# Block 0 alone ahead, blocks 1 to 3 together, and gathered rows asked for earlier than they are used

## The chip, the cores and the metric

The kernel runs on one core of a Trainium2 chip. The metric is the device time of one launch in microseconds. Of the engines, PE is TensorE (matmuls and transposes), DVE is VectorE, ACT is ScalarE, POOL is GpSimd, which here only sends the gathers of expert rows, and SP is the engine whose queue sends nearly all other transfers. Each engine works through its own list of instructions in a fixed order; a wait in front of one instruction holds back everything behind it on that engine.

## The reference

One decoder block over 512 tokens of width 1024, in float32. Two mixers run on one projection, their outputs are merged, and a layer of 16384 one-neuron experts follows:

```
h    = rms_norm(x); parts = split(h @ w_in)
y_att = sparse attention: an indexer picks 128 causal keys a query, softmax over these
y_dn  = chunked gated DeltaNet (conv, l2 norm, decay, triangular solve, state over chunks)
merged = sigmoid(ga) * (y_att @ w_att) + sigmoid(gb) * (y_dn @ w_dn)
x    = x + merged @ w_o
h2   = rms_norm(x); q = h2 @ w_query              # 8 heads, 2 halves of 128
s    = q . sub_keys; top 16 of 128 in each half   # the "lists"
best 16 of the 256 sums -> expert number, gate = softmax(best)
x    = x + sum over 8 heads x 16 experts: gate * gelu(u[e] . h2) * v[e]
```

## The kernel before, in words

The 512 tokens are four blocks of 128. The last step, the experts, is done in two ways. Blocks 0 and 1 (`SINGLE`) fetch for each token and each of its 128 picks the row `u[e]`, and later the row `v[e]`: one gather brings one row for each of 128 tokens (128x1024 float32, 512 KB), so a block needs 128 gathers for u and 128 for v, 512 in all. VectorE then makes a dot product with `h2` (line 923, called the use of a u row) or adds the row times its coefficient to `x1` (line 934, the use of a v row). Blocks 2 and 3 (`WHOLE`) go over all 16384 experts densely: `dense_u` multiplies a 128x1024 tile `ut` with the transposed `hT1` of both blocks (8 matmuls of 256 columns), `spread` turns picks and gates into a dense table of gates in DRAM (`gd`), and `dense_v` multiplies the activations, times those gates, with the v tiles into the accumulators `acc`. Fifty-four of the 128 `dense_u` are made ahead of `dense_v`, the rest beside it.

In front of that lie four chains (two of `deltanet`, `indexer`, `attender`), which go over the blocks in order. Between their steps a filler (`fill`) hands out other work: the projections (`hr` is the normed input of blocks 1 to 3, transposed, so its matmuls have 384 columns), and then `path`, which is merge, `w_o`, second norm, queries, scores and lists of the blocks that it is given. `path` runs three times: for block 0 and for block 1 alone in `single(b)` inside the filler, and for blocks 2 and 3 together after the chains. `choose` makes the final 16 picks of a head out of the lists, by top-8 passes on VectorE.

What sets the order: the functions are generators, and how many steps of the filler go between two steps of the chains is a constant (`FILL_A`, `FILL_B`). In the filler every second step also emits one row (`STEPS`), in the last `path` every second step (`STEPS_E`), in `spread` four a chunk (`CHUNK_ROWS`), in `dense_v` a share that comes from the work done. The framework then fixes each engine's order once, when the program is built. `all_rows` gives out the rows: u of block 0, u of block 1, v of block 0, v of block 1, each with its gather and its use together. Until the chains are over a row has one of four buffers (`ROWS`), then also one of eight more (`MORE_ROWS`). The expert numbers are `eu` (line 902), from which the v rows are had by adding 1 in place once the u rows are through.

Of the kernel before, what the change touches and what calls it, by code (L numbers as in the profile page):

```python
# [32 lines left out]
SINGLE, WHOLE = (0, 1), (2, 3)  # L33
NU = len(WHOLE) * P

FILL_A = 1.6
FILL_B = 1.8
# [10 lines left out]
AHEAD = 40  # L48
# [4 lines left out]
ROWS, MORE_ROWS = 4, 8  # L53
STEPS, STEPS_E, CHUNK_ROWS = 2, 2, 4
# [5 lines left out]
CST = ["ident", "triu", "ones", "blk64", "causneg", "causbias"] + [f"m{k}" for k in range(6)]  # L60
# [3 lines left out]
def constants():  # L64
# [5 lines left out]
        "ones": r >= 0,  # L70
# [15 lines left out]
def tile_block(ctx, tc, x, xT0, xT1, w_in, sc_cols, sc_rows, w_br, w_o, w_q, subT, uT, uv, cst, iota, out, dbg=None):  # L86
# [44 lines left out]
    hr = hp.tile([P, 8, NX], F32, name="hr")  # L131
# [24 lines left out]
    ident, triu, ones, blk64 = cs("ident"), cs("triu"), cs("ones"), cs("blk64")  # L156
# [84 lines left out]
    rowv = cp.tile([P, 8 + D], F32, name="rowv")  # L241
    load(rowv, sc_rows.to_broadcast([P, 8 + D]))
    alog, dtb, n2g = rowv[:, 0:4], rowv[:, 4:8], rowv[:, 8:8 + D]
# [274 lines left out]
    def projections(part):  # L518
# [17 lines left out]
        yield from output_gates(1)  # L536
        yield from keys(1)
        yield from queries(1)
        for t in (8 * br + dt for dt in range(8) for br in range(2)):
# [193 lines left out]
    x1d = {b: dr.tile([P, D], F32, name=f"x1d{b}") for b in (*SINGLE, *WHOLE)}  # L733
    uv2 = uv.rearrange("e (t d) -> (e t) d", t=2)
    x1, h2, ex_u, act = {}, {}, {}, {}
# [3 lines left out]
    def path(bs, place, banks=("mm",)):  # L739
# [10 lines left out]
        m_ = place("m", None)  # L750
        for dt in range(8):
            s_ = tmp()
            part = lambda t, i: t[:, i * n * P:(i + 1) * n * P]
            if bs[0] == 0:
# [9 lines left out]
            else:  # L764
                for i in range(2):
                    load(part(s_, i), sgd[8 * i + dt][:, slice(c.start - P, c.stop - P)])
                S.activation(s_[:, :2 * n * P], s_[:, :2 * n * P], AF.Sigmoid)
            w = plain(w_br[dt])
            o = turn()
            for i, y in enumerate((qT, szT)):  # L770
                for k in range(4):
                    mm(part(o, i), w[:, 4 * i + k, :], y[:, k, c], k == 0, k == 3)
                    if n > 1 and k == 1:
                        yield
                yield
            V.tensor_tensor(s_[:, :2 * n * P], s_[:, :2 * n * P], o[:, :2 * n * P], op=ALU.mult)
# [168 lines left out]
    def fill():  # L945
# [3 lines left out]
        while True:  # L949
# [19 lines left out]
            if not active:  # L969
                yield  # L970
# [288 lines left out]
```

## Time and profile before

| | us |
|---|---|
| three runs: lowest, median, highest | 1860.33, 1864.8, 1871.26 |
| the profiled execution's own time | 1860.58 |
| its span, from the first instruction to the last | 1858.8 |
| TensorE busy, VectorE busy | 1678.5, 1332.8 |
| ScalarE busy, GpSimd busy | 573.6, 629.4 |

Busy times are sums over the whole span; what an engine is worth in one stage has to be read from a window of that stage. The program falls into seven stages: the chains with the projections until the first gather is asked for (0 to 453 us), the chains with gathers beside them (to 718), the path of blocks 2 and 3 (to 854), `choose` for block 2 (to 938), the spread of both (to 1140), a gap (to 1201), and `dense_v` (to 1854). The last 4.8 us store the result.

### The profile page before, as it was taken

What the parts mean: (1) busy time and instruction counts of PE and PEld (TensorE: products, weight loads), DVE (VectorE), ACT (ScalarE), POOL (GpSimd) and SP (SyncE); (2) the same over time, 40 slices, a digit from 0 to 9 for tenths busy, and PEclk for the clock granted to TensorE, in tenths of its full rate; (3) what the DMA queues carried; (4) which work ended last, traced back from release to release, by engine and by line L of the source; (5) the groups of instructions that cost most, each with busy time, mean ns of one, the idle gap of its engine ahead of it and who ended that gap; (6) DMA issues with size and microseconds to landing.
All of it is one profiled execution on the core that took longest, in us unless ns stands there. A gap on an engine that the chain in (4) does not pass through costs nothing.

```text
span 1858.8 us, 24234 instructions
## 1 busy us (share of the span) xinstructions
PE 1678.5 (90%) x8330; PEld 1311.6 (71%) x8330; DVE 1332.8 (72%) x3114; ACT 573.6 (31%) x1165; POOL 629.4 (34%) x516
## 2 busy tenths in 40 slices
PE   6899999899999968895379997699999999999998
PEld 5766686776667766495269996477777777777766
DVE  3733563978678899789996877886865856567675
ACT  5255322221136314011056885011212222122222
POOL 0000000001542443446834435554533533343430
PEclk8999999999998987997779999799999999999999
DMA  5422355343998899999979999999998999999985
GB/s 212 137 102 74 111 193 195 100 142 106 338 328 319 310 361 336 363 343 360 366 271 343 359 366 389 412 409 409 404 373 325 410 354 365 395 365 362 383 312 170
DMA packets 190123, 556.30 MB, mean 299 GB/s; under 512 B 17840, under 2 KB 63664, under 8 KB 187952
## 3 DMA queue, kind: packets, MB, share of 16 engines
q1 hardware_dynamic: 116272, 286.28, 42.4%
q0 software_dynamic: 73728, 268.47, 38.3%
q8 instruction: 66, 1.08, 0.2%
q14 instruction: 57, 0.47, 0.1%
HBM read 528.60 MB, written 25.95 MB: 298 GB/s over the span
## 4 chain that ended last, share of the span: by engine, by line
PE 54%; DVE 15%; issue 12%; DMA 11%; POOL 5%; ACT 2%; DVEq 0%; POOLq 0%; SPq 0%; ACTq 0%
PE acc L94 18%; PE mm L94 14%; DMA row<-in_uv_dram,eu 9%; PE dn L94 5%; POOL row L913 4%; DVE row L923 3%; PE at L94 3%; DVE wk L573 1%; DVE m L572 1%; DMA row__9423<-in_uv_dram,eu 1%; DMA row__8663<-in_uv_dram,eu 1%; DMA row__7536<-in_uv_dram,eu 0%; DMA row__7605<-in_uv_dram,eu 0%; PE at L609 0%; DMA C<-in_cst_dram 0%
## 5 line engine op out<-in xcount | busy, mean ns | idle before, releaser
L913 POOL DMA_INDIRECT row<-in_uv_dram,eu x318 | 386.3, 1215 | 933.0 <-DVE eu L902 455.3
L923 DVE CUSTOM_DVE_ANT_0 row<-row,h 128x1024 f32<-128x1024 f32 x233 | 281.5, 1217 | 59.4 <-DMA row<-in_uv_dram,eu 58.6
L94 PE MATMUL mm<-hT,ut 128*128 128x256 f32 x864 | 204.5, 394 | 64.4 <-ACT ge L1058 34.2
L94 PE MATMUL mm<-hr,wt 128*128 128x384 f32 (+1 forms) x688 | 241.2, 490 | 0.0
L94 PEld LDWEIGHTS mm<-hT,ut 128*128 128x128 f32 x864 | 168.1, 199 | 89.7 <-ACT ge L1058 35.0
L180 DVE TENSOR_TENSOR vl<-vt,vh 128x1024 fp32r<-128x1024 f32 x86 | 104.0, 1220 | 103.9 <-ACT vh L179 103.8
L94 PEld LDWEIGHTS mm<-hr,wt 128*128 128x128 f32 x688 | 122.9, 190 | 75.9 <-issue 8.6
L94 PE MATMUL acc<-vt,ge 128*128 128x512 f32 x336 | 151.0, 592 | 0.0
L94 PE MATMUL acc<-vl,ch 128*128 128x512 f32 x344 | 139.6, 406 | 6.5 <-DVE vl L180 6.5
L94 PE MATMUL acc<-vh,cl 128*128 128x512 f32 x344 | 135.7, 394 | 0.0
L94 PE MATMUL acc<-vh,ch 128*128 128x512 f32 x344 | 121.9, 437 | 3.8 <-ACT gs L1054 3.8
L179 ACT CAST vh<-vt 128x1024 fp32r<-128x1024 f32 x86 | 88.1, 1044 | 85.7 <-DMA vt<-in_uv_dram 85.1
L934 DVE SCALAR_TENSOR_TENSOR x1s<-row,act,x1s 128x1024 f32<-128x1024 f32 x85 | 109.0, 1282 | 3.0 <-DMA row<-in_uv_dram,eu 1.3
L180 DVE TENSOR_TENSOR cl<-gt,ch 128x256 fp32r<-128x256 f32 x86 | 36.3, 423 | 101.2 <-ACT ch L179 97.9
L94 PEld LDWEIGHTS acc<-vt,ge 128*128 128x128 f32 x336 | 63.8, 190 | 62.6 <-issue 60.3
L179 ACT CAST ch<-gt 128x256 fp32r<-128x256 f32 x86 | 34.7, 404 | 231.9 <-PE acc L94 221.8
L94 PE MATMUL mm<-h,wt 128*128 128x128 f32 x624 | 82.4, 291 | 7.2 <-DVE h L202 4.3
L94 PEld LDWEIGHTS mm<-h,wt 128*128 128x128 f32 x624 | 79.3, 206 | 10.8 <-DVE h L202 4.6
L1098 ACT ACTIVATE ob<-ob,sl 128x128 f32<-128x128 f32 x256 | 78.2, 388 | 26.2 <-DVE ob L1095 26.2
L94 PEld LDWEIGHTS acc<-vh,ch 128*128 128x128 f32 x344 | 66.0, 192 | 26.0 <-issue 8.6
L94 PEld LDWEIGHTS acc<-vl,ch 128*128 128x128 f32 x344 | 65.3, 190 | 22.1 <-DVE vl L180 8.2
L94 PE MATMUL mm<-hT,wt 128*128 128x128 f32 x640 | 79.8, 284 | 1.0 <-ACT tmp L849 1.0
(988 smaller groups left out, 3189.8 us busy)
## 6 DMA issues: line engine op xcount, KB each, us to landing
ut<-in_uT_dram SPq DMA_DIRECT2D x128, 512.0 KB
vt<-in_uv_dram SPq DMA_DIRECT2D x128, 512.0 KB
wt<-in_w_in_dram SPq DMA_DIRECT2D x82, 512.0 KB
wt<-in_w_q_dram SPq DMA_DIRECT2D x48, 512.0 KB
gd<-gb SPq DMA_DIRECT2D x16, 1024.0 KB
gt<-gd SPq DMA_DIRECT2D x16, 1024.0 KB
wt<-in_w_br_dram SPq DMA_DIRECT2D x24, 512.0 KB
wt<-in_w_o_dram SPq DMA_DIRECT2D x24, 512.0 KB
```

Of the source, the lines that this page charges most:

```text
L94: hop[0] = PE.matmul(o, l, r, start=start, stop=stop).ins
L179: S.copy(hi, src)
L180: return V.tensor_tensor(lo, src, hi.bitcast(F32), op=ALU.subtract).ins
L572: V.max(m8, src[:, :N])
L573: V.match_replace(wk[:, :N], m8, src[:, :N], TAKEN)
L913: G.indirect_dma_start(out=r, out_offset=None, in_=uv2, in_offset=bass.IndirectOffsetOnAxis(ap=ix, axis=0))
L923: V.tensor_tensor_reduce(r, r, h2[b], 1.0, 0.0, op0=ALU.mult, op1=ALU.add, accum_out=act[b][:, s:s + 1])
L934: V.scalar_tensor_tensor(x1[b], r, act[b][:, s:s + 1], x1[b], op0=ALU.mult, op1=ALU.add)
L1098: S.activation(ob[:, t], ob[:, t], AF.Copy, scale=sl[:, 2, n:n + 1])
```

## The change

- `path` runs twice, for block 0 alone and for blocks 1 to 3 together. `single(1)` is gone from the filler, so `w_br`, `w_o` and `w_q` are loaded twice and not three times; matmuls of the later `path` have 384 columns where they had 256, and 128 in `single(1)`.
- In the filler, block 0's `path` goes ahead of all projections once its chains are done, and until then the filler gets fewer steps (`FILL_0` 0.9 where it was 1.6).
- Rows are handed out in the order block 0 u, block 0 v, block 1 u, block 1 v, 0.3 a step of the filler, and each gather is emitted three (later seven) rows ahead of the use that belongs to it. There are five buffers, later six more a ring. The numbers of the v rows are a table of their own.
- Block 1's scores are kept; its lists, its `choose` and its expert numbers are written behind the spread of blocks 2 and 3 in the program.
- 52 `dense_u` are made ahead instead of 54; eight of these are left until behind the spread in the program.
- `norm2`'s gain is loaded into `h2` and not held all the time; `x1` of blocks 0 and 1 stays in SBUF.

The diff, cut to its core:

```
+OTHERS = (1, 2, 3)
-FILL_A = 1.6
-FILL_B = 1.8
+FILL_0, FILL_A, FILL_B = 0.9, 1.6, 1.8
-AHEAD = 40
+AHEAD = 38
-ROWS, MORE_ROWS = 4, 8
-STEPS, STEPS_E, CHUNK_ROWS = 2, 2, 4
+ROWS, MORE_ROWS = 5, 6
+PACE, STEPS_E, CHUNK_ROWS = 0.3, 3, 4
+LAGS = 3, 7
+LAST_U = 8
...
     def path(bs, place, banks=("mm",)):
...
             w = plain(w_br[dt])
-            o = turn()
+            ss = []
             for i, y in enumerate((qT, szT)):
+                s_ = tmp()[:, :N]
+                load(s_, sgd[8 * i + dt])
+                S.activation(s_, s_, AF.Sigmoid)
+                o = turn()[:, :N]
                 for k in range(4):
-                    mm(part(o, i), w[:, 4 * i + k, :], y[:, k, c], k == 0, k == 3)
+                    mm(o, w[:, 4 * i + k, :], y[:, k, c], k == 0, k == 3)
...
+                if n == 1 or b in WHOLE:
+                    lists(b, h, sc, place("sr", b))
+                else:
+                    kept[h] = sc
...
     def all_rows():
-
+        coming = []
         for b in SINGLE:
             while b not in act:
                 yield
-            for s in range(P):
-                r = row_of(ex_u[b][:, s:s + 1])
-                V.tensor_tensor_reduce(r, r, h2[b], 1.0, 0.0, ...)
-                emitted[0] += 1
-                yield
-        for b in SINGLE:
...
+            for second in range(2):
+                for s in range(P):
+                    coming.append((b, second, s, row_of(places[b][second][:, s:s + 1])))
+                    emitted[0] += 1
+                    if len(coming) > LAGS[len(rings) > 1]:
+                        use(*coming.pop(0))
+                    yield
+        for c in coming:
+            use(*c)
...
     def fill():
...
+            if alone is None and done >= {("y", 0, i) for i in range(3)}:
+                alone = single(0)
+            if SINGLE[0] in act:
+                due += PACE
+                while due >= 1.0:
+                    due -= 1.0
+                    rows()
+            if alone is not None and next(alone, True) is None:
+                pass
+            elif others and next(others[0], True):
+                others.pop(0)
+            yield
...
-            due += FILL_A if ("attention", 1) not in done else FILL_B
+            due += FILL_0 if ("y", 0, 0) not in done or ("y", 0, 1) not in done else FILL_A if ("attention", 1) not in done else FILL_B
...
-    while SINGLE[-1] not in act:
+    while SINGLE[0] not in act:
         next(filler)
...
-    for n, _ in enumerate(path(WHOLE, place, ("mm", "at", "dn0", "dn1"))):
+    for n, _ in enumerate(path(OTHERS, place, ("mm", "at", "dn0", "dn1"))):
...
-            dense(left * (NCH - n) // NCH)
+            dense(LAST_U + (left - LAST_U) * (NCH - n) // NCH)
             rows(CHUNK_ROWS)
+    dense(0)
+    b = SINGLE[1]
+    for h in range(8):
+        lists(b, h, kept[h], rp.tile([P, 2 * P], F32, name="sr1"))
+    choose(b, new)
+    indices(b, new, lp)
```

Three places where the order of instructions moves. VectorE, around the first expert numbers `eu0` and the first uses of u rows; before, rows (each with an instruction that reads its sum into `act0`) stand among single steps of the chains:

```order
L901 TENSOR_SCALAR area_2915<-area_2905 128x128
L902 SCALAR_TENSOR_TENSOR eu0_2991<-area_2905,area_2915 128x128
L923 ISA row_2995,act0_2994<-row_2995,h2_0_2093 128x1024
L923 ISA act0_2994 128x1
L923 ISA row_3038,act0_2994<-row_3038,h2_0_2093 128x1024
L923 ISA act0_2994 128x1
L923 ISA row_3051,act0_2994<-row_3051,h2_0_2093 128x1024
L923 ISA act0_2994 128x1
L417 TENSOR_TENSOR vb_3728<-dn0_3729,beta_139 128x256
L423 TENSOR_TENSOR attT_3767<-dn0_3768,dT_2999 128x256
L923 ISA row_3090,act0_2994<-row_3090,h2_0_2093 128x1024
L923 ISA act0_2994 128x1
```

After, a little behind `eu0`, the same engine has block 1's delta rule (`AT`, `am`, `XX`) between runs of rows:

```order
L954 ISA row_2330,act0_2258<-row_2330,h2_0_1716 128x1024
L954 ISA act0_2258 128x1
L385 TENSOR_TENSOR AT_2492<-dn1_2493,dT_2417 128x256
L391 TENSOR_TENSOR am_2514<-AT_2492,C_87 128x256
L393 TENSOR_TENSOR XX_2513<-C_87,am_2514 128x256
L954 ISA row_2336,act0_2258<-row_2336,h2_0_1716 128x1024
L954 ISA act0_2258 128x1
L954 ISA row_2356,act0_2258<-row_2356,h2_0_1716 128x1024
L954 ISA act0_2258 128x1
L954 ISA row_2363,act0_2258<-row_2363,h2_0_1716 128x1024
L954 ISA act0_2258 128x1
L954 ISA row_2400,act0_2258<-row_2400,h2_0_1716 128x1024
```

What moved is the point at which rows begin: `eu0` stands at row 778 of VectorE's order before and at row 528 after. From `eu0` to the last attention step of block 3 VectorE has 102 uses of rows before and 201 after.

TensorE, in the queries of the late path (`hT1` is its transposed, normed input, `sT` the keys of the scores); before, a query is done block by block:

```order
L94 MATMUL dn0_6264<-hT1_5619,wt_6265 128x128 x8
L94 MATMUL dn0_6264<-hT1_5619,wt_6267 128x128 x5
L94 MATMUL mm_6229<-sT_6225,qt_6227 128x128 x2
L94 MATMUL at_6248<-sT_6225,qt_6227 128x128 x2
L94 MATMUL dn0_6264<-hT1_5619,wt_6267 128x128 x3
L94 MATMUL dn0_6264<-hT1_5619,wt_6265 128x128 x8
L94 MATMUL dn0_6264<-hT1_5619,wt_6267 128x128 x8
```

After, one set of eight does three blocks:

```order
L98 MATMUL dn0_5836<-hT1_4985,wt_5838 128x384 x8
L98 MATMUL dn1_5837<-hT1_4985,wt_5851 128x384 x2
L98 MATMUL dn1_5796<-sT_5791,qt_5793 128x128
L98 MATMUL mm_5812<-sT_5791,qt_5793 128x128
L98 MATMUL at_5828<-sT_5791,qt_5793 128x128
L98 MATMUL dn1_5837<-hT1_4985,wt_5851 128x384 x6
```

The 256 narrow query matmuls of this path became 112 of 384 columns, 16 of 256 and 16 of 128.

VectorE where the spread starts (`oa`, `ob` are its one-hot tables); before, the rest of the second `choose` and uses of block 1's u rows (`act1`) follow the first tables:

```order
L1095 TENSOR_TENSOR oa_7303<-io_142,sl_7300 128x1024
L1095 TENSOR_TENSOR ob_7304<-io_142,sl_7300 128x1024
L1095 TENSOR_TENSOR oa_7327<-io_142,sl_7300 128x1024
L1095 TENSOR_TENSOR ob_7328<-io_142,sl_7300 128x1024
L704 TENSOR_SCALAR a__7987<-t1_7985 128x128
L709 TENSOR_SCALAR n__7996<-pf_7984 128x128
L692 TENSOR_REDUCE gs_7980<-gate3_5629 128x8
L923 ISA row_5861,act1_5191<-row_5861,h2_1_4401 128x1024
```

After, the same place has uses of block 0's v rows (into `x1_0`) and the candidate sums of block 1's `choose` (`ca` from `ts1`):

```order
L1121 TENSOR_TENSOR oa_6660<-io_144,sl_6657 128x1024
L1121 TENSOR_TENSOR ob_6661<-io_144,sl_6657 128x1024
L1121 TENSOR_TENSOR oa_6684<-io_144,sl_6657 128x1024
L1121 TENSOR_TENSOR ob_6685<-io_144,sl_6657 128x1024
L950 SCALAR_TENSOR_TENSOR x1_0_1715<-row__7381,act0_2258,x1_0_1715 128x1024
L693 MAX_INDEX bp_7215<-bs_7214,cr0_7252 128x8
L693 MAX_INDEX bp_7215<-bs_7214,cr1_7258 128x8
L695 TENSOR_TENSOR gate3_4994<-bs_7214 128x128
L677 TENSOR_TENSOR ca_8048<-ts1_5484 128x8x16
```

Block 1's `choose`, written behind the spread, was drawn into it, and the 256 rows of block 1 all stand behind it.

## Rows read from the trace of the kernel before

**Rows 1.** Windows of the seven stages; busy us and records of each engine.

```profile
core 0: us, PE busy (x) PEld busy (x) DVE busy (x) ACT busy (x) POOL busy (x), PEclk, DMA share, GB/s
0.00:453.00 453.00, 417.14 (x2355) 317.20 (x2356) 267.91 (x957) 155.73 (x313) 0.20 (x4) 0.97 0.40 135
453.00:718.00 265.00, 233.91 (x1256) 172.43 (x1255) 208.07 (x664) 88.52 (x180) 111.54 (x104) 0.92 0.91 327
718.00:854.00 136.00, 126.08 (x785) 105.68 (x785) 119.53 (x401) 20.65 (x39) 59.63 (x53) 0.95 0.95 346
854.00:938.00 84.00, 26.70 (x103) 21.39 (x102) 83.28 (x316) 7.89 (x15) 61.42 (x50) 0.68 0.94 354
938.00:1140.00 202.00, 196.34 (x1138) 179.25 (x1139) 163.02 (x222) 150.08 (x363) 93.06 (x68) 0.97 0.97 343
1140.00:1201.00 61.00, 35.56 (x149) 29.65 (x147) 44.39 (x48) 7.07 (x14) 34.48 (x29) 0.83 1.03 412
1201.00:1854.00 653.00, 642.65 (x2554) 485.98 (x2552) 445.35 (x510) 143.64 (x243) 269.08 (x212) 0.99 0.94 361
```

**Rows 2.** Timeline: start, length, engine, instruction, idle time before with its releaser.

```profile
409.43 0.61 PE L94 MATMUL mm<-tmp 128*128 128x128 f32 x4
...
455.17 0.29 DVE L902 SCALAR_TENSOR_TENSOR eu<-area 128x128 int32<-128x128 f32 x1
455.74 1.07 POOL L913 DMA_INDIRECT row<-in_uv_dram,eu  x1 [455.29 <-DVE eu L902]
...
461.26 1.22 DVE L923 CUSTOM_DVE_ANT_0 row<-row,h 128x1024 f32<-128x1024 f32 x1 [5.80 <-DMA row<-in_uv_dram,eu]
```

**Rows 3.** Groups of instructions: busy us, mean ns of one, idle before.

```profile
L923 DVE CUSTOM_DVE_ANT_0 row<-row,h 128x1024 f32<-128x1024 f32 x233 | 281.5, 1217 | 59.4 <-DMA row<-in_uv_dram,eu 58.6 <-issue 0.2
L94 PE MATMUL mm<-hT,ut 128*128 128x256 f32 x864 | 204.5, 394 | 64.4 <-ACT ge L1058 34.2 <-DMA ut<-in_uT_dram 30.2
L94 PE MATMUL mm<-hr,wt 128*128 128x384 f32 x496 | 173.9, 490 | 0.0
...
L934 DVE SCALAR_TENSOR_TENSOR x1s<-row,act,x1s 128x1024 f32<-128x1024 f32 x85 | 109.0, 1282 | 3.0 <-DMA row<-in_uv_dram,eu 1.3 <-DVE x1s L934 0.2
...
L94 PE MATMUL dn<-hT,wt 128*128 128x128 f32 x320 | 38.1, 279 | 0.0
L94 PE MATMUL mm<-wt,m 128*128 128x512 f32 x80 | 37.7, 596 | 0.0
```

**Rows 4.** Timeline of VectorE where uses of u rows follow each other directly.

```profile
892.89 1.22 DVE L923 CUSTOM_DVE_ANT_0 row__7761<-row__7761,h 128x1024 f32<-128x1024 f32 x1
894.04 0.08 DVE L923 DVE_READ_ACCUMULATOR2_ANT act<- 128x1 f32 x1
```

**Rows 5.** The same groups, VectorE up to 720 us: delta rule and top-8 passes.

```profile
L399 DVE TENSOR_TENSOR XX<-XX,dn 128x512 f32<-128x512 f32 x40 | 27.2, 681 | 19.1 <-PE dn L94 18.3 <-issue 0.6
L572 DVE MAX8 m<-wk 128x8 f32<-128x256 f32 (+2 forms) x45 | 24.9, 553 | 0.6
L573 DVE MATCH_REPLACE8 wk<-m,wk 128x256 f32<-128x256 f32 (+2 forms) x45 | 24.3, 540 | 0.0
```

**Rows 6.** Windows of 46 to 47 us; columns as in the first group.

```profile
650.00:696.00 46.00, 31.61 (x218) 28.43 (x219) 41.57 (x171) 5.43 (x15) 18.57 (x18) 0.87 0.98 362
696.00:743.00 47.00, 38.14 (x151) 30.38 (x150) 45.21 (x163) 19.24 (x27) 18.92 (x19) 0.70 0.94 336
882.00:929.00 47.00, 17.57 (x64) 14.02 (x62) 46.28 (x175) 4.30 (x7) 38.15 (x30) 0.72 0.97 366
```

**Rows 7.** Waits from 453 to 718 us: total us, times, longest.

```profile
POOL row L913 <- DVE act L923: 73.3, 42, 5.1
DVE row L923 <- DMA row<-in_uv_dram,eu: 42.0, 34, 5.8
```

**Rows 8.** Timeline in the gap between spread and `dense_v`, TensorE.

```profile
1170.99 12.51 PE L94 MATMUL mm<-hT,ut 128*128 128x256 f32 x48 [18.46 <-DMA ut<-in_uT_dram]
```

More of the change, by code (lines that the diff above doesn't have):

```diff
@@ L58 @@
 PLAIN = 3
-CST = ["ident", "triu", "ones", "blk64", "causneg", "causbias"] + [f"m{k}" for k in range(6)]
+CST = ["ident", "triu", "blk64", "causneg", "causbias"] + [f"m{k}" for k in range(6)]
 CI = {n: i for i, n in enumerate(CST)}
@@ L69, in constants @@
         "triu": r <= c,
-        "ones": r >= 0,
         "blk64": (r // 64) == (c // 64),
@@ L750, in path @@
         m_ = place("m", None)
+        N = n * P
         for dt in range(8):
-            s_ = tmp()
-            part = lambda t, i: t[:, i * n * P:(i + 1) * n * P]
-            if bs[0] == 0:
+            if n == 1:
+                s_, o = tmp(), None
+                part = lambda t, i: t[:, i * P:(i + 1) * P]
                 o = turn()
@@ L830, in path @@
         for h in range(8):
+            o = first_o
             if h:
-                o = turn()
-                w = [plain(w_q[2 * h + p]) for p in range(2)]
-                for j in range(n):
-                    for p in range(2):
-                        yield from query(o, w[p], j, p)
-            else:
-                o = first_o
+                o = [turn() for _ in range(2)] if n > 1 else [turn()] * 2
+                for p in range(2):
+                    yield from query(o, plain(w_q[2 * h + p]), p, slice(0, N))
             sT = place("sT", None)
@@ L914, in row_of, with use @@
         return r
+    def use(b, second, s, r):
+        a = act[b]
+        if second:
+            V.scalar_tensor_tensor(x1[b], r, a[:, s:s + 1], x1[b], op0=ALU.mult, op1=ALU.add)
+            if s == P - 1:
+                nc.sync.dma_start(out[col(b), :], x1[b])
+            return
+        V.tensor_tensor_reduce(r, r, h2[b], 1.0, 0.0, op0=ALU.mult, op1=ALU.add, accum_out=a[:, s:s + 1])
+        if s == P - 1:
+            S.activation(a, a, AF.Gelu)
+            V.tensor_tensor(a, a, flat(gate[b]), op=ALU.mult)
     def all_rows():
+        coming = []
         for b in SINGLE:
@@ L945, in fill @@
     def fill():
-        active, singles, n, b = [projections(0)], list(SINGLE), 0, None
-        nexts = [projections(1)]
+        others, alone, due = [projections(0), projections(1)], None, 0.0
         while True:
-            if b is None and singles and done >= {("y", singles[0], i) for i in range(3)} and (singles[0] == 0 or not nexts and len(active) == 0):
-                b = singles.pop(0)
-                active.append(single(b))
-            if nexts and len(active) == 0 or nexts and done >= {("z", 0)}:
-                active.insert(0, nexts.pop(0))
-            if SINGLE[0] in act and n % STEPS == 0:
-                rows()
-            n += 1
-            for g in active + active[1:]:
-                if g not in active:
-                    continue
-                try:
-                    next(g)
-                except StopIteration:
-                    active.remove(g)
-                    if b in act:
-                        b = None
-                    continue
-                yield
-            if not active:
-                yield
+            if alone is None and done >= {("y", 0, i) for i in range(3)}:
[9 more added lines that the diff above has]
+                others.pop(0)
+            yield
     sgd = [dr.tile([P, T - P], F32, name=f"sgd{t}") for t in range(16)]
```

122 lines of the change are left out of this document (63 added, 59 removed).

## The prediction

> **What bounds the kernel now.** First the windows by stage. Two stages are TensorE's almost alone, `dense_v` with 642.65 of 653 us and the spread with 196.34 of 202; in both VectorE has 40 to 200 us to spare. The path (718 to 854) is nearly so: 126.08 of 136. `choose` (854 to 938) is VectorE's: 83.28 of 84, TensorE 26.70. The gap (1140 to 1201) belongs to the transfers, 412 GB/s with TensorE at 35.56 of 61 [rows 1]; there the last `dense_u` wait 18.46 us for `ut` [rows 8]. The chain stage with rows (453 to 718) is mixed: TensorE 233.91 of 265 and VectorE 208.07, that is 88% and 79% [rows 1]. The finer windows say which of them is near its end: VectorE fills 90% of 650 to 696 and 96% of 696 to 743, TensorE 69% and 81% [rows 6]. So as soon as rows are dense, VectorE is what the chains wait for. The change leaves the late stages much as they are and doubles the rows in just this stage, so the question is what that does to the chains' end.
>
> **The change, part by part.** I set it against the profiled execution: 1858.8 us of span and 1.8 outside it, 1860.6, which is 4.2 under the median of the runs. Counts come from the two built orders, durations from the rows.
>
> *When rows can begin.* Before, the last score matmul of block 0 is at 409.43 and its numbers `eu` are ready at 455.17 + 0.29, 46 us later, filled with top-8 work [rows 2]. TensorE has fewer matmuls ahead of that score after: 72 of 384 columns and not 200, 214 small ones of the delta rule and not 312, 58 of attention and not 89. By 0.70 us each (173.9 over 248; a float32 matmul is two records) and 0.24 (38.1 over 160) [rows 3] that is 128 x 0.70 + 129 x 0.24 = 121 us of work; TensorE is busy 417.14 of 453 [rows 1], so 131 us of time. The score comes at 278, and the first request 46 later at about 325. The bounds are 300 (the 46 us shrink to 21, if block 0 is alone on VectorE) and 335 (no gain from the idle share).
>
> *The chains with rows beside them.* From `eu0` to the last attention step of block 3, VectorE's order holds 201 uses of rows after, 102 before. The 128 u rows cost 1.15 each (892.89 to 894.04 back to back [rows 4]), 147; the 73 v rows 1.28 [rows 3], 93. Since `eu0` stands earlier, 148 us of chain work now lie behind it too. Its largest term is the indexer's top-8 passes: 48 pairs at 0.553 + 0.540 [rows 5], less 0.07 of overlap an instruction, 46; then the delta rule at 48 (23 products `XX` at 0.68 are 16 of that [rows 5]), attention 16, small inverse roots 15, index sums 14, and 11 of the rest. The same way of counting gives 205 for the stretch before, where the trace has 208.07 [rows 1]. So VectorE has 147 + 93 + 148 = 388 us of work, while TensorE has some 305. At the share that VectorE reaches when rows are dense, 0.933 (41.57 + 45.21 over 93 [rows 6]), this takes 416 us, and the chains end at 325 + 416 = 741; before it was 718. At 0.99, which only `choose` has (46.28 of 47 [rows 6]), it is 717; at 0.90, 756. Filling `single(1)` out of this stage does take 59 us from TensorE, but TensorE isn't late here.
>
> *The gathers' latency.* A gather's use came 5.5 us after its request [rows 2], and before VectorE waited 42.0 us for rows in this stage, over about 100 of them, 0.4 each [rows 7]. Requests there waited 73.3 us for a buffer [rows 7]. Now a gather is asked for three rows ahead, into five buffers. If four rows of other work (4.6 us and more) lie between, little remains; if the wait stays, 201 x 0.4 = 80 us come on top. I take none at the forecast, since the shares above already hold a part of it, and keep 80 for the range. By the Trainium skill ("DMA: Bandwidth & Descriptors", Anatomy of one DMA, SWDGE path) such a transfer takes 2.0 us and its bytes at 436 GB/s, an estimate of 3.2 us for 512 KB. Five buffers would then hide it wholly. The trace's 5.5 us is over that, so the page does not settle it.
>
> *The path.* It now carries block 1 too. After the chains' end TensorE has 16 more `w_o` matmuls at 0.94 [rows 3], 15; queries of 112 x 0.70 + 16 x 0.474 + 16 x 0.24 = 90 where there were 256 x 0.24 = 61, 29; branches 48 x 0.70 against 64 x 0.474, 3; scores and transposes 6. That is 53 on a stage which TensorE fills to 93%: 136 + 53 = 189. Thirty-two weight loads of 512 KB fewer and 28 fewer gathers (53 GpSimd records before [rows 1]) leave the transfers lighter, but they weren't what was late.
>
> *`choose`.* The same VectorE work for two blocks with some 30 rows beside it, where there were about 41: 84 - 11 x 1.2, with 6 to 9 us back for the two heads' chains standing closer: 80. *The spread.* 296 `dense_u` matmuls beside it and not 312, -16 x 0.474 = -8; against it block 1's `choose`, some 17 us of VectorE, which has 39 idle now and 42 rows fewer, so nothing; ScalarE bunched at the end, +5. I take 200. *The gap.* It was long because gathers and the v tiles took the queues from the last `ut`. After, no row of block 1 is asked for until its numbers are there, behind the spread. I take 38 and keep 61 as a bound.
>
> *`dense_v`.* 576 `dense_u` matmuls and not 592, -8: 645 by TensorE. All 256 gathers of block 1 now lie here, where 212 did [rows 1]. The bytes are 361 x 0.653 = 236 MB before, plus 44 x 0.524, 258 MB: 626 us at the gap's 412 GB/s. It is close to the end of what is there; behind the last `dense_u`, some 109 us of TensorE have 58 MB to bring in, 141 us, of which buffers and an uneven order hide a part. I add 12: 657. The Trainium skill ("DMA: Bandwidth & Descriptors", Where 436 GB/s comes from) puts transfers between HBM and SBUF at about 358 GB/s. By that this stage would need 258 / 0.358 = 721 us. The trace says no: 412 over the whole gap, and 361 over `dense_v` itself.
>
> *Sum.* 741 + 189 + 80 + 200 + 38 + 657, with 4.8 behind it and 1.8 outside the span: 1911.6, say 1912. That is 51 over the profiled execution: +23 in the chains, +53 in the path, -25 in the four stages behind it. The work that `single(1)` did in idle time of a stage now stands where TensorE has none.
>
> **The rivals.**
> 1. *VectorE has more room than I give it.* If only TensorE's work counts, the chains end at 718 - 59 = 659 and the whole at 1830. For it: VectorE idles 57 us in the stage before. Against it: 388 us from 325 to 659 don't fit. It needs the first request at 300, a full VectorE (692) and 10 to 20 us won in the path by its lighter transfers: 1840 to 1855. Faster.
> 2. *It cancels.* The first request is at 300, VectorE at 0.99 throughout: 300 + 392 = 692, and the sum is 1863. No change that a measurement of this kernel can tell (within 0.5%, 1855.5 to 1874).
> 3. *The gathers make VectorE wait.* The 0.4 us of each row stays with five buffers, for all 201: the chains end at 325 + 388 + 80 = 793, and the time is 1964. For it: 42.0 us of waits before [rows 7], and 201 x 0.524 MB with the weights ask for about 330 GB/s over the stage, as much as the 327 of before. Against it: the requests are further ahead of the uses. With half of the wait it is 1935 to 1940.
> 4. *The end waits for transfers.* The 58 MB behind the last `dense_u` take their 141 us in full: 20 us on the forecast, 1932. Inside the range.
>
> **How the numbers follow.** The forecast (chains' end at 717 to 756) has 0.50, with 1885 to 1930 as its own range; rival 4 has 0.06, rival 3 0.17, rival 2 0.14 and rival 1 0.13. Slower by over 0.5% is forecast, 3 and 4: 0.73. Same 0.14, faster 0.13. The range of 8 in 10 leaves out the better part of rival 1 and the upper half of rival 3: 1850 to 1960.
>
> **What the profile after would show.** The first gather at 300 to 335 us. From there to the last attention copy VectorE at 90% or more and TensorE well under 80%, ended near 740. The next stage near 190 us, TensorE over 90%. A gap under 45 us, and `dense_v` with the transfers' share near 1.0 in its last quarter. The forecast is wrong if the chains end before 705 us, or if the path takes under 170; the size is wrong through rival 3 if VectorE's waits for rows are over 60 us before the chains end.

## The result, and the profile after

The changed kernel takes 1930.0 us (four runs, 1926.3 to 1933.3) against 1864.7 of the kernel before: a ratio of 1.035, with a 95% interval of 1.031 to 1.039. It is 3.5% slower. The forecast was 1912. The profiled execution took 1927.2 us over a span of 1925.3.

The windows by stage, cut at these events: first gather, last attention copy, last score, first and last spread matmul, first and last `acc`.

```profile
core 0: us, PE busy (x) PEld busy (x) DVE busy (x) ACT busy (x) POOL busy (x), PEclk, DMA share, GB/s
0.00:318.00 318.00, 287.01 (x1805) 237.40 (x1806) 168.78 (x662) 116.59 (x242) 0.20 (x4) 0.96 0.49 164
318.00:762.00 444.00, 353.36 (x1385) 228.21 (x1383) 387.84 (x872) 94.27 (x212) 230.40 (x206) 0.82 0.83 294
762.00:938.00 176.00, 172.45 (x600) 103.60 (x600) 74.25 (x396) 28.96 (x66) 4.20 (x5) 0.98 0.36 118
938.00:1016.00 78.00, 58.61 (x244) 49.68 (x245) 77.89 (x266) 10.74 (x23) 45.97 (x35) 0.89 0.95 349
1016.00:1210.00 194.00, 188.81 (x1108) 172.72 (x1106) 119.17 (x213) 148.79 (x361) 22.95 (x15) 0.99 0.75 239
1210.00:1231.00 21.00, 14.56 (x67) 12.04 (x65) 3.11 (x4) 5.28 (x8) 0.00 (x0) 1.00 0.97 317
1231.00:1921.00 690.00, 649.96 (x2520) 481.46 (x2520) 491.36 (x692) 144.80 (x245) 327.91 (x252) 0.97 0.95 367
```

Two cuts of [rows 1] lie a little ahead of their events: in the kernel before the first gather is at 456 us and the last attention copy at 720, not at 453 and 718. By the events, the chains end 42 us later (762, 720), the path is 42 longer (176, 134), `dense_v` 37 longer (690, 653); the gap is 40 shorter (21, 61), spread and `choose` 8 and 6 shorter. That sums to 67, the difference of the two executions. The column of POOL tells where the gathers went: 206 before the chains' end, 5 in the path, 35, 15 and none in the next three stages, 252 in `dense_v`. So while the path runs, the transfers move 118 GB/s and VectorE is busy 74 of 176 us; both are crowded before and behind it.

In the chain stage TensorE has long holes. The longest, on TensorE's timeline (start, length, instruction, idle time before it with what ended it):

```profile
429.43 0.39 PE L98 MATMUL dn<-vn,attT 128*128 128x128 f32 x2
466.94 1.64 PE L98 MATMUL at<-ikT,iqT 64*128 64x384 f32 x2 [37.13 <-DVE mx L604]
468.52 2.29 PE L98 MATMUL mm<-hr,wt 128*128 128x384 f32 x3
```

For 37 us TensorE stands before a matmul that needs the bank `at`; behind it in the order are projections, which then start without a wait. The bank is freed by the first attention step of block 1 on VectorE (`mx`). VectorE's timeline shows why that comes so late:

```profile
434.71 0.08 DVE L579 MATCH_VALUE_LOAD wk<-m,wk 128x8 f32 x1
434.78 0.40 DVE L579 MATCH_REPLACE8 wk<-m,wk 128x256 f32<-128x256 f32 x1
435.11 0.15 DVE L346 TENSOR_SCALAR s<-s 128x2 f32<-128x2 f32 x1
435.18 1.21 DVE L954 CUSTOM_DVE_ANT_0 row<-row,h 128x1024 f32<-128x1024 f32 x1
436.32 0.08 DVE L954 DVE_READ_ACCUMULATOR2_ANT act<- 128x1 f32 x1
436.32 0.16 DVE L177 TENSOR_SCALAR rs_t<-s 128x2 int32<-128x2 int32 x1
436.39 1.21 DVE L954 CUSTOM_DVE_ANT_0 row<-row,h 128x1024 f32<-128x1024 f32 x1
...
462.66 0.42 DVE L581 SCALAR_TENSOR_TENSOR bias<-wk,acc 128x256 f32<-128x256 f32 x1
...
464.64 0.29 DVE L582 TENSOR_SCALAR bias<-bias 128x256 f32<-128x256 f32 x1
...
466.47 0.42 DVE L604 CUSTOM_DVE_ANT_0 t<-at,bias 128x256 f32<-128x256 f32 x1
```

The indexer's top-8 passes are a serial chain (`wk`, then `m`, then `wk`), and so is the inverse root (`s`, `rs_t`, `r`). Between two links of 0.15 to 0.4 us stand one or two uses of rows of 1.2 us. The window of the hole:

```profile
429.00:467.00 38.00, 0.87 (x9) 0.68 (x7) 34.58 (x94) 1.12 (x3) 28.93 (x23) 0.56 0.88 302
```

VectorE is busy 34.58 of the 38 us, and yet the chain on which TensorE waits crawls: `bias`, its end, comes at 462.66, the attention at 466.47, TensorE at 466.94.

### The profile page after: what moved, and what is told of

It is laid out like the page before. It is cut to its first block, busy times and chain, and to the rows that moved or that the text cites. A ratio compares the mean times of both kernels' runs of the same rounds, so it can differ in the third digit from the quotient of the medians.

```text
span 1925.3 us, 22897 instructions
## 1 busy us (share of the span) xinstructions
PE 1724.8 (90%) x7722; PEld 1285.1 (67%) x7722; DVE 1323.2 (69%) x3101; ACT 549.4 (29%) x1151; POOL 631.6 (33%) x516
## 3 DMA queue, kind: packets, MB, share of 16 engines
q1 hardware_dynamic: 108208, 267.86, 39.3%
q0 software_dynamic: 73728, 268.47, 37.7%
## 4 chain that ended last, share of the span: by engine, by line
PE 42%; DVE 21%; issue 19%; DMA 11%; POOL 4%; ACT 2%; SPq 0%; DVEq 0%; POOLq 0%; ACTq 0%
PE mm L98 11%; PE acc L98 10%; PE dn L98 7%; DVE row L954 4%; PE at L98 4%; DMA row<-in_uv_dram,eu 3%; DVE x L950 3%; POOL row L943 2%; DMA row<-in_uv_dram,ev 2%; DVE wk L579 1%; DMA row__10808<-in_uv_dram,ev 1%; DMA row__8436<-in_uv_dram,eu 1%; DVE m L578 1%; DMA row__11766<-in_uv_dram,ev 1%; DMA vt<-in_uv_dram 1%
## 5 line engine op out<-in xcount | busy, mean ns | idle before, releaser
L943 POOL DMA_INDIRECT row<-in_uv_dram,eu x171 | 200.4, 1172 | 451.8 <-DVE r L182 319.3
L98 PE MATMUL mm<-hr,wt 128*128 128x384 f32 (+1 forms) x688 | 246.0, 501 | 0.5 <-issue 0.5
L954 DVE CUSTOM_DVE_ANT_0 row<-row,h 128x1024 f32<-128x1024 f32 x171 | 208.1, 1221 | 25.5 <-DMA row<-in_uv_dram,eu 25.1
L943 POOL DMA_INDIRECT row<-in_uv_dram,ev x133 | 163.3, 1228 | 154.2 <-DVE x L950 98.9
L98 PE MATMUL mm<-hT,ut 128*128 128x256 f32 x832 | 191.3, 388 | 16.6 <-ACT ge L1084 10.8
L98 PEld LDWEIGHTS mm<-hT,ut 128*128 128x128 f32 x832 | 159.4, 195 | 39.2 <-ACT ge L1084 11.4
L950 DVE SCALAR_TENSOR_TENSOR x<-row,act,x 128x1024 f32<-128x1024 f32 x133 | 170.0, 1278 | 4.0 <-DMA row<-in_uv_dram,ev 3.2
L98 PE MATMUL acc<-vl,ch 128*128 128x512 f32 x344 | 144.6, 420 | 24.3 <-DVE vl L186 24.0
L98 PE MATMUL acc<-vh,ch 128*128 128x512 f32 x344 | 112.2, 432 | 8.5 <-ACT vh L185 4.6
L1121 DVE TENSOR_TENSOR oa<-io,sl 128x1024 f32<-128x1024 f32 x32 | 38.9, 1217 | 68.5 <-PE dn L98 68.5
```

Source lines behind the costliest of these rows:

```text
L98: hop[0] = PE.matmul(o, l, r, start=start, stop=stop).ins
L943: G.indirect_dma_start(out=r, out_offset=None, in_=uv2, in_offset=bass.IndirectOffsetOnAxis(ap=ix, axis=0))
L950: V.scalar_tensor_tensor(x1[b], r, a[:, s:s + 1], x1[b], op0=ALU.mult, op1=ALU.add)
L954: V.tensor_tensor_reduce(r, r, h2[b], 1.0, 0.0, op0=ALU.mult, op1=ALU.add, accum_out=a[:, s:s + 1])
L1121: V.tensor_tensor(o_, io[:, None].to_broadcast([P, TB, P]), which, op=ALU.is_equal)
```

## The experiments

All stages in one table, from the profiled executions, in us, cut at the events; the time is the median of the runs, with its ratio to the kernel before; "uses" is the number of row uses that VectorE's order holds from `eu0` to the last attention step, the last two columns are gathers.

| kernel | time (ratio) | first gather | chains' end | path | choose | spread | gap | dense_v | uses | in path | in dense_v |
|---|---|---|---|---|---|---|---|---|---|---|---|
| before | 1864.7 | 456 | 720 | 134 | 84 | 201 | 61 | 653 | 102 | 51 | 211 |
| changed | 1930.0 (1.035) | 318 | 762 | 176 | 78 | 194 | 21 | 689 | 201 | 4 | 252 |
| e1 held | 1902.7 (1.020) | 319 | 725 | 186 | 78 | 202 | 21 | 689 | 139 | 56 | 252 |
| e2 light uses | 1811.7 (0.972) | 319 | 601 | 216 | 78 | 193 | 22 | 689 | light | 68 | 252 |
| e3 no lag | 1913.6 (1.026) | 320 | 762 | 176 | 78 | 189 | 20 | 681 | 201 | 4 | 245 |
| e4 choose1 mid | 1923.0 (1.032) | 316 | 757 | 176 | 78 | 208 | 21 | 676 | 201 | 4 | 212 |
| e5 spread out | 1876.6 (1.007) | 315 | 696 | 184 | 91 | 223 | 24 | 649 | 119 | 74 | 198 |
| e6 rush | 1930.6 (1.036) | 319 | 758 | 176 | 78 | 195 | 20 | 692 | 201 | 4 | 252 |
| e7 FILL_0 1.6 | 1856.2 (0.996) | 392 | 654 | 195 | 80 | 199 | 20 | 702 | 126 | 46 | 277 |
| e8 before, light | 1845.9 (0.991) | 455 | 718 | 133 | 66 | 158 | 111 | 654 | light | 55 | 216 |
| e9 after top-8 | 1952.8 (1.050) | 316 | 649 | 264 | 77 | 191 | 22 | 741 | 61 | 71 | 317 |
| e10 fill, mid, no lag | 1849.3 (0.992) | 394 | 661 | 196 | 80 | 211 | 24 | 681 | 126 | 46 | 238 |
| e11 fill, mid, held | 1835.0 (0.984) | 393 | 646 | 186 | 93 | 218 | 25 | 663 | 109 | 74 | 209 |
| e12 FILL_0 1.6, light | 1811.5 (0.971) | 393 | 592 | 214 | 80 | 187 | 22 | 706 | light | 76 | 277 |

**e1: the path's rows held in the path.** In the program 60 rows are written into the late path, but nothing ties them to it, and the order has them all in front of the chains' end. Here they follow the path's own VectorE steps (`behind(x)` keeps what is written in it behind the instruction `x`).

```
-            rows()
+            with behind(vhop[0] if n else None):   # vhop: the path's last VectorE step
+                rows()
```

> The 60 rows that the program writes into the late path, and that VectorE's order has in front of the chains' end, are held behind the path's own VectorE steps: 139 uses of rows and not 201 from eu0 to the last attention step. Theory A (VectorE's row work, in its fixed order, stretches the chains): 62 x 1.21 = 75 us less VectorE work there, so at the share of 0.874 that the stage has now the chains end at 318 + 313/0.874 = 676, between 665 and 700 us where they end at 762 now; the path, with VectorE idle for 100 of its 176 us, takes 176 to 186; the whole is 1855 to 1880. Rival B (the gathers' latency makes VectorE wait): the waits for rows are 25 us over the stage, so the 62 rows carry some 8 us, and the time stays above 1910. Rival C (only the path's size counts): no change of the chains' end by more than 20 us.

Measured 1902.7 us, chains' end 725, path 186. Rivals B and C are out, but theory A had forecast at least twice the gain (50 to 75 us where 27 came). The rows that were taken away are the last ones of the stage, and the hole of 37 us at 430 us is as long as before (37.7).

**e2: light uses.**

```
+        if len(rings) == 1:
+            V.tensor_tensor(a[:, s:s + 1], r[:, 0:1], r[:, 1:2], op=ALU.mult)
...
+            return
```

> Every gather stays, but the uses of rows that are emitted until the late path ends work on single columns (0.1 us and not 1.2): the u sums and v additions of those rows are left out. Theory A: VectorE has some 150 us of work beside the chains and TensorE 305, so TensorE sets the pace and the chains end at 650 to 675 us, and no wait of TensorE for VectorE is over 10 us; the time is 1820 to 1850. Rival B (latency or transfers): the same gathers keep the chains' end above 735.

Measured 1811.7 us; the chains end at 601, below what was forecast, and TensorE has no wait left to speak of:

```profile
319.00:601.00 282.00, 277.83 (x1263) 178.76 (x1262) 168.45 (x647) 87.93 (x198) 133.67 (x142) 1.00 0.93 336
601.00:818.00 217.00, 200.17 (x722) 123.19 (x720) 93.54 (x487) 33.13 (x75) 66.63 (x70) 0.95 0.71 261
```

The first row is the chain stage, the second the path. TensorE is busy 98% of the first at a granted clock of 1.00, while the transfers run at 336 GB/s, more than the 294 of the changed kernel (142 gathers in 282 us, 206 in 444). So neither the gathers' latency nor their bytes hold up the chains; VectorE's work on the rows does. It costs 118 us of time: 161 at the chains' end, less 40 that the path takes back, because matmuls that ran beside the chains now stand in it (722 records, 600 in the changed kernel). Over both stages TensorE has the same work, 1985 records in both kernels, and is busy with it for 478 us here and 526 there, where the granted clock of the chain stage was 0.82.

**e3: no lag.** `-LAGS = 3, 7` and `+LAGS = 0, 0`.

> LAGS 0 and 0: a gather and its use are written together, as before the change. Theory A: the lag decides little, since the number of uses in each stage is the same; waits for rows in the chain stage rise from 25 to 40 to 80 us, of which TensorE sees a part: 1925 to 1960. Rival B: with the latency bare again the time goes above 1970.

Measured 1913.6 us: a miss with the other sign, the lag costs 16 us. The early stages are the same to 2 us; the gain lies behind them, spread 5 and `dense_v` 8. In the changed kernel the queue of gathers shows the price:

```profile
1086.15 1.06 POOL L943 DMA_INDIRECT row<-in_uv_dram,eu  x1 [0.30 <-issue]
1232.23 1.21 POOL L943 DMA_INDIRECT row__8213<-in_uv_dram,eu  x1 [145.03 <-DVE x L950]
```

With a lag of seven, block 0's last seven uses are written only when the next seven rows are given out, which are those of `dense_v`. Until then their buffers are taken: four gathers of block 1 go out before the spread's end, and then none for 145 us. Without the lag eleven go out, and the queue still stands for 119 us; `dense_v` has seven gathers fewer. Nor did the lag hide latency: beside the chains VectorE waits 28.4 us for rows without it and 28.1 with it.

**e4: block 1's choose between the spreads, six rows a chunk.**

```
+        if b == WHOLE[1]:
+            for h in range(8):
+                lists(SINGLE[1], h, kept[h], rp.tile([P, 2 * P], F32, name="sr1"))
+            choose(SINGLE[1], new)
+            indices(SINGLE[1], new, lp)
...
-    choose(b, new)
-    indices(b, new, lp)
```

> Block 1's lists, choose and numbers are written between the spreads of blocks 2 and 3, and six rows a chunk are handed out there: 40 more rows are used before dense_v, 223 and not 263 behind it. Theory D (dense_v is 37 us longer than before because all 256 rows of block 1 lie in it): 40 x 0.524 = 21 MB and 50 us of VectorE less there, so dense_v goes from 690 to 660 to 670, the spread from 194 to 195 to 205, and the time to 1895 to 1915. Rival E (dense_v is longer through TensorE's clock or its own order, not through rows): dense_v stays above 680 and the time at 1925 to 1940.

Measured 1923.0 us, `dense_v` 676, spread 208: half of what theory D had. Forty gathers fewer give back 13 us of `dense_v` and cost 14 in the spread; the whole is 7 us better, and 5 of these lie in the chains, which the edit does not touch.

**e5: several steps together.** The edits of e1, e3 and e4, and `PACE, STEPS_E, CHUNK_ROWS = 0.25, 2, 6`.

> Several steps together: rows of the late path held behind its own VectorE steps and given every second step, 0.25 rows a filler step, no lag, and block 1's choose between the two spreads with six rows a chunk. VectorE's order then has 119 uses of rows before the chains' end (201 in the changed kernel), 210 behind the spread (263). Theory A (about 0.85 us a row, worked out from 762, 725 and 601 us at 201, 139 and no full uses): chains' end at 695 to 710, path 195 to 205, spread 205 to 212, dense_v 670 to 680, in all 1880 to 1900. Rival (the stall of 37 us at 430 us and the slower clock behind it decide, not the number of rows): the chains end above 725 and the time is over 1905.

Measured 1876.6 us: the chains' end, 696, is in the range of the forecast, path (184) and `dense_v` (649) are better, the spread (223) is worse, and `choose` grew to 91. It is still 0.7% over the kernel before. The hole is still there (39.3 us), in a kernel whose chains end 66 us sooner: so it does not decide the chains' end alone, and the rival is out.

**e6: a quarter more rows a step beside dense_v.** `spent` became `1.25 * spent` in its loop.

> Only the pace of rows beside dense_v is changed: a quarter more rows a step, so that they are through before the last fifth of it. Theory F (dense_v loses its time at the end, where u rows, the Gelu and 128 serial v rows of block 1 run until 15 us before the end and TensorE stands 29 us in the last 190): dense_v goes from 689 to 665 to 678 and the time to 1912 to 1922. Rival G (the transfers are full from the start, 386 GB/s in the first 100 us, so pulling rows forward only moves the waits): dense_v stays at 685 to 700.

Measured 1930.6 us, `dense_v` 692: no change. The rows did end sooner (the last gather at 1810 us, not at 1892), and in its last 89 us TensorE is busy for 87 where it was for 74; but it stands more in the 600 us before that (561 and 576 busy). Theory F is not borne out and rival G is: handing rows out sooner moves the waits and does not shorten the stage.

**e7: FILL_0 alone undone.**

```
-FILL_0, FILL_A, FILL_B = 0.9, 1.6, 1.8
+FILL_0, FILL_A, FILL_B = 1.6, 1.6, 1.8
```

> FILL_0 at 1.6, the number that the kernel before had for these steps: the filler no longer waits for block 0's chains. The first gather goes from 318 to 390 to 430 us, with 126 uses of rows before the chains' end and 288 behind the spread. Theory A: with 75 rows fewer beside them the chains end at 710 to 740; dense_v, with 25 rows more, takes 695 to 715; the time is 1905 to 1935, so this part of the change is worth little either way. Rival H (the early start of block 0 is what the change loses by): chains' end under 700 and a time under 1890.

Measured 1856.2 us: 74 us better than the changed kernel, and 0.4% under the one before (0.994 to 0.999). Rival H came out and theory A did not; this was the miss that settled the case. The first gather comes 74 us later and the chains end 108 us sooner. Where the top-8 passes lie tells why. One line of the `wk` tile from each profile (passes, shortest/median/longest ns, first and last start); the kernel before:

```profile
L572 DVE MAX8 m<-wk x45: 419/545/696, 254.8 to 435.1; 128x8 f32<-128x256 f32 x15, 128x8 f32<-128x384 f32 x15, 128x8 f32<-128x512 f32 x15
```

The changed kernel:

```profile
L578 DVE MAX8 m<-wk x45: 404/552/696, 393.1 to 704.1; 128x8 f32<-128x256 f32 x15, 128x8 f32<-128x384 f32 x15, 128x8 f32<-128x512 f32 x15
```

With FILL_0 at 1.6:

```profile
L578 DVE MAX8 m<-wk x45: 418/560/695, 226.3 to 497.8; 128x8 f32<-128x256 f32 x15, 128x8 f32<-128x384 f32 x15, 128x8 f32<-128x512 f32 x15
...
L581 DVE SCALAR_TENSOR_TENSOR bias<-wk,acc x2: 418/484/549, 246.8 to 284.3; 128x256 f32<-128x256 f32 x1, 128x384 f32<-128x384 f32 x1
```

The instructions are no slower, 545, 552 and 560 ns. But in the kernel before all of them are over before the first gather (456). With 0.9 all three blocks' passes begin behind the first gather (318) and take until 704. With 1.6 those of two blocks are over by 284 (`bias`, which ends a block's passes), before the first gather at 392. At 0.9 the projections that feed the indexer come later, and so its whole serial work falls into the stage with rows.

**e8: the kernel before with light uses of u rows.** The same cut as in e2, in its own loop.

> The kernel before, with the same cut as in the light run: u rows that are emitted until its late path ends are used on single columns, so their sums are left out. Theory A: in the kernel before, rows cost the chains little, because there were 102 and TensorE was busy for 88%: the chain stage goes from 265 to 235 to 250 us and the path from 136 to 125 to 135, in all 1815 to 1840 against 1863. So the two kernels without this row work lie within 30 us of each other (1812 for the changed one), and the 67 us between them is rows. Rival C (the joint path and the order of blocks cost by themselves): the kernel before falls below 1790.

Measured 1845.9 us: chains' end and path as they were (718 and 133, from 720 and 134); the gain is in `choose` and spread, and the gap gives most of it back (111). So in the kernel before the rows beside the chains cost next to nothing: theory A's forecast for the chain stage, 235 to 250 us, missed (263), and rival C is out too. Without this row work the changed kernel is 34 us faster than the kernel before, a little over the 30 of the expectation (the cut takes 222 uses out of VectorE's order there and 201 in e2).

**e9: rows only behind the last top-8 pass.**

```
-            if SINGLE[0] in act:
+            if SINGLE[0] in act and last_mask:
...
-                    rows()
+                    with behind(last_mask[0]):
+                        rows()
```

> The changed kernel with FILL_0 still 0.9, but beside the chains rows are handed out only behind the last top-8 pass of the indexer on VectorE: 61 uses before the chains' end instead of 201, 65 in the path, and 328 behind the spread. Theory J (the early start of block 0 leaves the indexer's serial top-8 passes of blocks 1 to 3 in the stage with rows, where every link waits for a row; the attention and TensorE's order wait for them): the three passes run as in the light run, from 390 to 410, to about 475 and to 545 us, where they run from 391 to 709 now; no wait of 37 us on TensorE; the chains end at 610 to 640. dense_v is over-full with 328 gathers, 720 to 765, so the time is 1845 to 1890. Rival H (the early start costs through the projections that it delays, rows or not): the passes still end behind 600 us and the chains behind 690.

The mechanism came out as theory J had it, the time did not (1952.8 us). The passes run again as in the light run:

```profile
L578 DVE MAX8 m<-wk x45: 421/560/695, 387.5 to 539.8; 128x8 f32<-128x256 f32 x15, 128x8 f32<-128x384 f32 x15, 128x8 f32<-128x512 f32 x15
```

The chains end at 649 and 1.4 us of waits for `mx` are left. But the rows come back in one crowd at the start of the path:

```profile
649.00:745.00 96.00, 52.34 (x164) 36.22 (x165) 79.75 (x164) 6.88 (x15) 72.25 (x55) 0.60 0.89 313
745.00:913.00 168.00, 162.71 (x579) 97.70 (x578) 84.51 (x414) 26.84 (x63) 18.00 (x18) 1.00 0.46 166
```

For 96 us VectorE is busy 83%, TensorE 55% at a granted clock of 0.60, and most of its waits are for VectorE's `ot` and `XX` (17.5 and 13.7 us). From 775 to 905 no gather is sent, and over the second window TensorE runs at 97%. And 317 gathers are left for `dense_v`, which takes 741 us.

**e10 and e11: the steps that helped, together.** e10 is FILL_0 1.6 with the edits of e3 and e4; e11 has e1's as well and `STEPS_E` 2.

> Three steps that each gave time alone: FILL_0 1.6, no lag, block 1's choose between the spreads with six rows a chunk; 249 uses behind the spread and not 288. The early stages stay as with FILL_0 alone (392, 262, 195, 80 us); spread 205 to 212; dense_v from 702 to 670 to 685; in all 1835 to 1848, under the kernel before. If the gains overlap, 1850 to 1858.

> As the run before it, and the path's rows held behind its own VectorE steps, every second step: 109 uses before the chains' end (126), 113 in path and choose (76), 220 behind the spread (249). Chains' end at 635 to 648, path 200 to 210, choose 85 to 92, spread 212 to 222, dense_v 650 to 662: 1820 to 1840. If the path has no room for 37 more rows, it takes over 215 us and the time is no better than the run before it.

Measured 1849.3 us (0.992, interval 0.989 to 0.995; its profiled execution was the longest of its runs, 1859.2) and 1835.0 us (0.984, 0.981 to 0.988). e10 lies between its two forecasts, gains that add up (1835 to 1848) and gains that overlap (1850 to 1858); e11 is in its range. Both are under the kernel before, e11 by 1.6%, and e11 is 5% under the changed one. The stages of e11:

```profile
0.00:393.00 393.00, 364.69 (x2197) 286.55 (x2198) 241.16 (x883) 140.86 (x299) 0.20 (x4) 0.98 0.43 145
393.00:646.00 253.00, 230.96 (x991) 152.91 (x990) 209.75 (x539) 67.98 (x151) 141.05 (x114) 0.91 0.86 308
646.00:833.00 187.00, 171.93 (x603) 104.20 (x601) 156.38 (x453) 31.41 (x68) 90.22 (x74) 0.96 0.85 307
833.00:925.00 92.00, 59.18 (x243) 49.52 (x243) 89.49 (x315) 11.86 (x23) 58.98 (x45) 0.83 0.94 349
925.00:1143.00 218.00, 186.26 (x1044) 166.98 (x1044) 181.99 (x298) 144.98 (x354) 139.88 (x71) 0.95 0.95 331
1143.00:1168.00 25.00, 21.36 (x98) 17.88 (x96) 2.91 (x4) 7.45 (x13) 0.00 (x0) 1.00 1.02 340
1168.00:1831.00 663.00, 643.16 (x2552) 482.69 (x2552) 440.12 (x613) 145.16 (x246) 276.12 (x209) 0.99 0.92 349
```

The transfers' share is 0.85 or more from the first gather to the end, and VectorE no longer has a stage with 60% to spare beside one without any: 83%, 84%, 97%, 83%.

**e12: FILL_0 1.6 with light uses.** e7's line and e2's.

> FILL_0 1.6 and, as in the light run, the uses of rows emitted until the late path ends on single columns (sums and additions of those rows left out). It tells apart why FILL_0 0.9 loses 74 us. Theory J (only together with rows: it brings block 0's rows in front of the indexer's and delta rule's steps of the other blocks): without row work the chains end where they do with 0.9, at 601 us, within 15, and the time is within 20 us of 1812. Rival H (0.9 delays the projections and with them the chains, rows or not): the chains end 25 us or more before 601, at 540 to 576.

Measured 1811.5 us, chains' end 592 and not 601. Without row work the two settings are the same to 9 us at the chains' end and to less than 1 in the time. So rival H, that the later projections cost by themselves, is out: FILL_0 costs its 74 us only together with the rows. The windows agree. VectorE does 169 us of work before the first gather in e2 and 168 from there to the chains' end; in e12 nearly the same work is split 240 and 85:

```profile
0.00:392.00 392.00, 363.81 (x2195) 286.04 (x2195) 240.43 (x880) 140.30 (x298) 0.20 (x4) 0.98 0.42 144
392.00:590.00 198.00, 191.43 (x837) 123.01 (x838) 85.01 (x370) 64.42 (x138) 92.68 (x98) 0.98 0.93 338
```

## Why the prediction was right, and where its sizes were off

The sign and the cause in the chain stage were right: VectorE's row work in front of the chains' end, with chain work that the early start leaves behind `eu0`. Point by point, forecast and measured: first gather 325 and 318; chains' end 741 and 762; path 189 and 176; `choose` 80 and 78; spread 200 and 194; gap 38 and 21; `dense_v` 657 and 690; in all 1912 and 1927 for this execution. That the sum is off by only 15 is partly luck: chains and `dense_v` came out 54 us longer than forecast, the four other stages 38 shorter.

*The chains.* The work was sized well: 388 us forecast, 387.84 measured (the terms listed for the 148 us of chain work add up to 150, which changes nothing). The term that was mis-sized is the share: 0.933 forecast for the whole stretch, 387.84/444 = 0.873 measured. Up to 702 us VectorE is busy 352 of 384, a share of 0.917. In the last 60 us, in which its rows run out (the last use starts at 733), it is busy for 36:

```profile
702.00:762.00 60.00, 46.90 (x180) 32.60 (x178) 35.57 (x76) 21.34 (x40) 20.57 (x17) 0.64 0.49 170
```

Here serial steps go to and fro between the engines: of VectorE's 56 idle us in the stage 24 lie in these 60, mostly behind TensorE and ScalarE. The prediction took VectorE as one pool of work; the pool has no place for the order of the chains in it, which the hole of 37 us shows best, VectorE busy and TensorE idle. That the hole and the tail belong together, TensorE's work being pushed to the end, is plausible and was not tested. TensorE's granted clock, 1.00 in the 48 us from 366, was 0.56 in the hole, near the lower of its two levels, and 0.82 over the stage ([rows 1]: 0.92). Rival 3 was wrong as a mechanism: VectorE waited 24.9 us in 128 uses of u rows and 3.2 in 73 of v rows, together less than the 42.0 in about 100 uses of [rows 7].

```profile
PE at L98 <- DVE mx L604: 37.9, 3, 37.1
DVE row L954 <- DMA row<-in_uv_dram,eu: 24.9, 26, 5.5
```

*The path.* The prediction booked the path's +53 us as the change's largest loss, "where TensorE has none". That step fails as an account, though 176 us was nearly its size (TensorE's work there grew by 46 us, 126.08 to 172.45, and not by 53). In e2 and e12, with light uses, chains and path together end at 818 and 807, in e8, with the same cut in the kernel before, at 851. So giving block 1 to the late path is no loss by itself: what the path gains in length the chains can lose. In the changed kernel the rows keep them from it; in e11, with its rows, chains and path end at 832, in the kernel before at 854.

*The gap and dense_v.* The gap fell further than forecast; no gather runs in it now, but whether that alone did it no run tells apart. `dense_v` was undersized by 33 us, the largest miss. TensorE was idle for 40 of its 690 us, [rows 1] 10 of 653. Its last 190 us:

```profile
1731.00:1831.00 100.00, 87.22 (x299) 57.41 (x297) 79.42 (x93) 22.47 (x34) 50.91 (x40) 0.95 0.94 360
1831.00:1921.00 90.00, 74.15 (x244) 47.29 (x244) 68.71 (x74) 19.58 (x28) 32.20 (x24) 0.92 0.83 315
```

The prediction looked for the loss in full transfers at the end (its term of 12 us, and the sign of a share near 1.0 in the last quarter). The share was 0.94 and 0.83, so this step fails. What TensorE waits for is mostly `vl`, the low part of a v tile, which VectorE makes out of `vt` and ScalarE's `vh`. The waits of the whole stage in the changed kernel, and two of them in e9, with the most gathers:

```profile
PE acc L98 <- DVE vl L186: 24.0, 7, 8.4
PE acc L98 <- DMA vt<-in_uv_dram: 10.3, 6, 3.4
DVE vl L186 <- ACT vh L185: 78.1, 34, 7.6
...
PE acc L98 <- DVE vl L186: 66.6, 18, 7.8
DVE vl L186 <- ACT vh L185: 23.7, 10, 7.6
```

With 198, 209, 252, 277 and 317 gathers in the stage (e5, e11, changed, e7, e9) TensorE's wait for `vl` is 5.5, 10.4, 24.0, 38.6 and 66.6 us. Its wait for `vt` stays between 2 and 11 in all changed kernels, and `vl`'s own wait for its input does not grow but falls (82, 84, 78, 49, 24). This points to VectorE, whose uses of rows stand in front of `vl`, rather than to late `vt` transfers; no run took the uses alone out of the stage.

The runs give a price. With 198, 209, 212, 238, 245, 252, 277 and 317 gathers in it, `dense_v` took 649, 663, 676, 681, 681, 689, 702 and 741 us: from end to end 92 us for 119 gathers, 0.77 each (other runs with 252 and 277 took 689 to 692 and 706). By that, as an estimate, the 41 gathers more than before would make 32 of the 36 us. But at nearly the number of the kernel before (211 gathers, 653 us, TensorE idle for 10), e11 took 663 with 209 and e4 676 with 212, TensorE idle for 20 and 22; so 10 to 23 us are not the number of gathers, and what they are stays open. The Trainium skill ("DMA: Bandwidth & Descriptors", Where 436 GB/s comes from) would hold transfers from HBM to about 358 GB/s; here, on one core, they moved 367 over the 690 us, and 412 in the gap of [rows 1], so the trace does not bear that out.

*What was not foreseen.* That FILL_0 alone carries more than the whole loss (74 of 65 us), and that the lag costs 16 us and hides no waits. With FILL_0 undone the other parts of the change together are worth 0.4%; which of them gain and which lose was tried only for the lag, for block 1's `choose` and for the rows of the late path. The prediction counted the work that the early start leaves behind `eu0` (148 us, with 240 of rows) and put no price on the order in which the two stand. Of the 108 us that e7 ends the chains sooner, part is that fewer uses stand beside them (126, 201). The nearest to a test of the position alone is e5 against e11, which have the same edits but for FILL_0 (0.9, 1.6) and the pace (0.25, 0.3), with 119 and 109 uses: chains' end 696 and 646, time 1876.6 and 1835.0. At e5's 0.85 us a row the ten uses are 8 or 9 us, so some 41 of the 50 us are the position; this is an estimate, and e5 against e7 gives the same 42.

## What to carry to other kernels

On an engine with a fixed order, filler work has two prices: its busy time, and the latency that it adds to every serial chain among whose links it is put. Before filler is started earlier, count how much of the engine's critical serial work will then lie behind its start; here 72 us of VectorE's work moved behind (240 us stand before the first gather in e12, 169 in e2). Without row work that cost no time that the runs show (1811.7 us in e2, 1811.5 in e12); with it 74 us were lost, of which some 40, as an estimate, go with the position, and 75 more uses beside the chains are part of the rest. And work that is only written into a later stage does not stay there when the order is made by readiness: tie it to a step of that stage, on its engine, and read from a window by stage whether it came there.

## What the runs showed of the hardware

A use of a u row on VectorE (128x1024) did not become slower with 206 gathers in the chain stage instead of 104 (mean 1219 ns in both), and the waits for rows there fell (28.1 us, 42.0). The transfers were not what held the chains: at 336 GB/s in e2 TensorE was busy 98% of the stage. A stretch of 96 us in which TensorE is busy 55% shows a granted clock of 0.60 (e9), and the same 1985 matmul records of chains and path cost 526 us of TensorE's busy time in the changed kernel, with 0.82 granted in the chain stage, and 478 in e2, with 1.00.
